# Eight backward mLSTM states beside the Hyena convolution, and the decay applied as the state product leaves its bank

## The chip, the cores and the metric

The kernel runs on one core of a Trainium2 chip. A core has five engines with queues of their own: TensorE (PE, matrix products into the PSUM banks), VectorE (DVE), ScalarE (ACT), GpSimd (POOL, which does not touch PSUM here) and SyncE (SP, which here only issues DMAs). PEld stands for the weight loads of TensorE. The metric is the device time of one execution in microseconds; lower is better.

## The reference

One encoder layer over a sequence of 2048 tokens and 1024 channels. Half of the mixer is a Hyena group (a long two-sided convolution by FFT, applied twice), the other half an mLSTM with four heads of 128 channels, run once forward and once backward over the sequence and summed. Cross-attention into 256 memory tokens, an MLP and norms follow. The part that the change touches is the chunkwise mLSTM; for one direction and one chunk:

```python
def step(carry, inp):
    C, n, m = carry
    qc, kc, vc, ic, fc = inp
    F = jnp.cumsum(fc, axis=-1)
    logw = F[..., :, None] - F[..., None, :] + ic[..., None, :]
    logw = jnp.where(lower, logw, -jnp.inf)
    log_inter = F + m[..., None]
    m_t = jnp.maximum(log_inter, jnp.max(logw, axis=-1))
    w = jnp.exp(logw - m_t[..., None])
    inter = jnp.exp(log_inter - m_t)
    s = jnp.einsum('bhtd,bhsd->bhts', qc, kc) * w
    num = jnp.einsum('bhts,bhse->bhte', s, vc) + inter[..., None] * jnp.einsum('bhtd,bhde->bhte', qc, C)
    den = jnp.sum(s, axis=-1) + inter * jnp.einsum('bhtd,bhd->bht', qc, n)
    h = num / jnp.maximum(jnp.abs(den), jnp.exp(-m_t))[..., None]
    ...
    C_new = carry_decay[..., None, None] * C + jnp.einsum('bhs,bhsd,bhse->bhde', we, kc, vc)
```

The backward direction is the same on the flipped sequence. `inter` is one number for each token and head: the decay by which the product of the queries with the incoming state is scaled.

## The kernel before

The kernel works on chunks of 128 tokens, so there are 16. A state is a 128x129 matrix for each head: column 129 is the normaliser, since the values carry a 129th column of ones (`va`).

The program is written as generators that yield a cost, and `weave` interleaves two of them by those costs; a planner then orders the instructions of each engine. `keep_in_program_order` (often called `pin`) holds an instruction at its place in the written order. In `program`:

- `hyena` (the convolution) is woven with the rest of the input projection (`sweep`, `natural`), with `gates`, which `among` advances by one step after every fourth step of the last sweep, and with the first five steps of `memproj` (`take(n, 5)`), which projects the memory keys and values for attention.
- Then the rest of `memproj` is woven with 20 steps of `mlstm`: 15 backward state updates and the first forward chunks. One more step follows.
- Then `attention` is woven with the remaining forward chunks, and `ffn` ends the kernel.

`gates` computes for all chunks and both directions, from the gate pre-activations, two rows for each direction, chunk and head (`negM`, the negated running maximum, and `inter`, the decay), which it stores to DRAM as `rows` (L1044, L1045), and four sets of columns, turned by TensorE and kept on chip as `cols` (L1052 to L1056).

`mlstm` opens its SBUF pool `m_sb` where the convolution's pool `h_sb` lay, so its first loads wait for the convolution's last tiles. It first runs the backward states from chunk 15 to chunk 1 (L1111 to L1120): load the chunk's keys (`kn`) and values (`va`), weight the values on POOL (`ve`), four products into two PSUM banks (L1102), add to the decayed old state on DVE (L1108; L1104 for the first chunk), and store the state to DRAM as `cbd` (L1118).

The forward loop then takes chunk after chunk. `loads` (L1122) fetches queries, transposed keys, the backward state `cbn`, values and rows, each row broadcast to all 128 partitions (tile `rw`, L1124, 256 KB a load): `negM` for each direction and `inter` where a state comes in. `scores` makes the score product, multiplies the queries by the decay row on POOL (L1156), adds the mask on POOL (L1157), takes the exponential on ACT (L1159) and multiplies by the scores on DVE (L1160). For each direction and pair of heads the products of the weights with the values (L1188) and of the scaled queries with the state (L1190) accumulate in one PSUM bank; ACT takes the absolute value of the normaliser (L1193), DVE forms the divisor and the output (L1196 to L1205).

PSUM banks come from two rings of four: `mm` for the large products, `hy` for the convolution, the mLSTM and attention's transposes. A take from a ring waits until the bank's last reader is done.

Of the kernel before, what the change touches and what calls it, by code (L numbers as in the profile page):

```python
# [9 lines left out]
F32 = mybir.dt.float32  # L10
# [122 lines left out]
class Prog:  # L133
# [821 lines left out]
    def gates_open(self, es):  # L955
        self.mcp = es.enter_context(self.tc.tile_pool(name="m_c", bufs=1, side="right"))
        self.gcols = self.mcp.tile([128, 4, 128], F32, name="cols")

    def gates(self):
        nc, tc = self.nc, self.tc  # L960
        gt = self.dram("gt", (L, 16))
        rows = self.dram("rows", (2, 128, 128))
        cols, pin = self.gcols, tc.keep_in_program_order
        with tc.tile_pool(name="m_g", bufs=1, side="right") as sg:
# [79 lines left out]
            nc.sync.dma_start(out=rows[0], in_=negM)  # L1044
            nc.sync.dma_start(out=rows[1], in_=inter)  # L1045
# [10 lines left out]
            nc.vector.tensor_copy(cols.rearrange("p a r -> p (a r)"), pt)  # L1056
        yield 1

    def mlstm(self, es):
# [4 lines left out]
        vd = self.dram("vd", (L, CH)).rearrange("(n s) c -> s n c", s=128)  # L1064
        od = self.dram("od", (L, CH)).rearrange("(n s) c -> s n c", s=128)
        ym = self.dram("ym", (L, CH))
        rows = self.dram("rows", (2, 128, 128))
# [3 lines left out]
        GC, EC, WC, DC = (cols[:, i] for i in range(4))  # L1071
# [10 lines left out]
        def bc(t, r):  # L1082
            return t[:, r:r + 4].unsqueeze(2).broadcast_to([128, 4, 129])

        def load(n, tag, src, bufs=2):
            t = sb.tile([128, 4, 128], F32, tag=tag, name=tag, bufs=bufs)
            nc.sync.dma_start(out=t.rearrange("p h d -> p (h d)"), in_=src[:, n])
            return t

        def load_v(n):  # L1090
            t = sb.tile([128, 4, 129], F32, tag="va", name="va", bufs=2)
            nc.sync.dma_start(out=t[:, :, 0:128], in_=vd[:, n].rearrange("s (h d) -> s h d", h=4))
            nc.vector.memset(t[:, :, 128:129], 1.0)
            return t

        def update(new, old, kk, va, r, eng):
            ve = sb.tile([128, 4, 129], F32, tag="ve", name="ve", bufs=2)
            eng.tensor_tensor(ve, va, bc(WC, r), ALU.mult)
            for p in range(2):
                pc = self.hy()  # L1100
                for i in range(2):
                    nc.tensor.matmul(pc[:, 129 * i:129 * i + 129], kk[:, 2 * p + i], ve[:, 2 * p + i], start=True, stop=True)  # L1102
                if old is None:
                    nc.vector.tensor_copy(new[:, 2 * p:2 * p + 2].rearrange("d h e -> d (h e)"), pc[:, 0:258])  # L1104
                    continue
# [826 lines left out]
```

## Time and profile before

| | us |
|---|---|
| median of 3 runs | 3234.75 (3233.29 to 3247.62) |
| profiled execution | 3234.7 |
| its span, first to last instruction | 3232.7 |

| engine | busy us | share of the span |
|---|---|---|
| PE | 3061.6 | 95% |
| PEld | 2442.4 | 76% |
| DVE | 2033.0 | 63% |
| ACT | 1506.0 | 47% |
| POOL | 1181.1 | 37% |

Busy time is an average over stages with different limits, so the stage has to be looked at and not the total. A busy TensorE is not TensorE at its peak: the granted clock (PEclk) says how fast it was allowed to run. In lists of transfers and products a name stands for a tile (`rw<-rows` is a load of the tile `rw` from the DRAM tensor `rows`), L1102 for line 1102 of the kernel, SPq for the queue of SyncE. Matmuls on 32-bit floats show as two instructions each.

### The profile page before, as it was taken

To read this page: it belongs to the slowest core of one execution; us is meant where nothing else is said; L and a number is where in the kernel's file an instruction comes from. 1 tells how busy PE (TensorE), PEld (TensorE's weight loads), DVE (VectorE), ACT (ScalarE), POOL (GpSimd) and SP (SyncE) were. 2 spreads that over 40 slices of the span, in tenths; PEclk is the share of its full clock that TensorE was granted. 3 is DMA by queue.
4 is the path that set the end of the run, shared out by engine and by line. 5 is a ranking of instruction groups with operands and counts; after the bars stand their busy time and mean duration, and the time that the engine had idled before them with its cause. 6 is when DMAs were issued, how large, how long until landed. Compare 5 with 4: busy or idle time off the path is not lost.

```text
span 3232.7 us, 45325 instructions
## 1 busy us (share of the span) xinstructions
PE 3061.6 (95%) x15241; PEld 2442.4 (76%) x15241; DVE 2033.0 (63%) x3535; ACT 1506.0 (47%) x2874; POOL 1181.1 (37%) x818
## 2 busy tenths in 40 slices
PE   6999999999999875999999998999999999999998
PEld 5655566776668764898988896888788887888876
DVE  7775366345865754776775556656755675556695
ACT  5533366434674333555453445555555543333335
POOL 0122012100111334324141207776855483434483
PEclk9999999999999996999999999999999999999999
DMA  5564776686666898667484537665644475444434
GB/s 191 186 208 161 248 203 201 178 274 177 194 198 191 274 301 270 204 186 251 132 286 140 186 99 238 210 210 162 216 149 152 160 243 159 137 135 149 125 95 166
DMA packets 451632, 617.71 MB, mean 191 GB/s; under 512 B 39614, under 2 KB 247614, under 8 KB 450376
## 3 DMA queue, kind: packets, MB, share of 16 engines
q1 hardware_dynamic: 415268, 556.31, 55.6%
q10 hardware_dynamic: 36132, 58.51, 5.4%
q8 instruction: 121, 1.98, 0.3%
q14 instruction: 111, 0.91, 0.1%
HBM read 416.47 MB, written 198.21 MB: 190 GB/s over the span
## 4 chain that ended last, share of the span: by engine, by line
PE 75%; DMA 10%; DVE 7%; issue 3%; ACT 2%; POOL 2%; SPq 1%; ACTq 0%; DVEq 0%; POOLq 0%
PE mm L340 16%; PE mm L338 16%; PE mm L339 16%; PE hy L340 5%; PE hy L338 5%; PE hy L339 5%; PE hy L175 3%; PE hy L873 1%; PE mm L842 1%; DMA rw<-rows 1%; PE hy L915 1%; DMA xt<-in_x_t_dram 1%; DVE wl L343 1%; PE hy L1188 1%; DVE bl L1505 1%
## 5 line engine op out<-in xcount | busy, mean ns | idle before, releaser
L343 DVE TENSOR_TENSOR wl<-wn,wh 128x512 fp32r<-128x512 f32 (+1 forms) x364 | 278.7, 802 | 116.6 <-ACT wh L343 116.0
L1505 DVE TENSOR_TENSOR bl<-wr,bh 128x512 fp32r<-128x512 f32 x213 | 236.8, 1118 | 132.0 <-ACT bh L1504 131.8
L1504 ACT CAST ah<-w 128x512 fp32r<-128x512 f32 x284 | 176.2, 622 | 299.8 <-PE hy L339 149.4
L920 POOL TENSOR_TENSOR b<-b,a 128x512 f32<-128x512 f32 x64 | 86.7, 1355 | 595.5 <-ACT b L918 454.9
L343 ACT CAST wh<-wn 128x512 fp32r<-128x512 f32 (+1 forms) x364 | 208.5, 617 | 180.6 <-PE mm L339 51.1
L338 PE MATMUL mm<-xh,wh 128*128 128x512 f32 x640 | 271.9, 426 | 3.0 <-ACT xh L498 2.6
L1505 DVE TENSOR_TENSOR al<-w,ah 128x512 fp32r<-128x512 f32 x236 | 225.0, 955 | 57.2 <-ACT ah L1504 56.8
L339 PE MATMUL mm<-xl,wh 128*128 128x512 f32 x640 | 256.9, 402 | 2.3 <-DVE xl L343 2.0
L340 PE MATMUL mm<-xh,wl 128*128 128x512 f32 x640 | 256.7, 401 | 0.0
L1504 ACT CAST bh<-wr 128x512 fp32r<-128x512 f32 x232 | 143.6, 621 | 234.7 <-PE mm L340 180.0
L340 PE MATMUL mm<-bh,al 128*128 128x512 f32 x576 | 225.3, 394 | 7.7 <-DVE al L1505 5.1
L338 PE MATMUL mm<-bh,ah 128*128 128x512 f32 x576 | 226.6, 393 | 0.1
L339 PE MATMUL mm<-bl,ah 128*128 128x512 f32 x576 | 225.6, 392 | 0.0
L338 PE MATMUL mm<-act,wh 128*128 128x512 f32 x512 | 199.5, 393 | 1.2 <-ACT wh L343 1.2
L339 PE MATMUL mm<-act,wh 128*128 128x512 f32 x512 | 200.3, 391 | 0.0
L340 PE MATMUL mm<-act,wl 128*128 128x512 f32 x512 | 199.0, 392 | 0.3 <-DVE wl L343 0.3
L1361 POOL TENSOR_TENSOR ssum<-ssum,sq 128x512 f32<-128x512 f32 x56 | 81.1, 1448 | 289.5 <-ACT sq L1360 289.5
L338 PE MATMUL hy<-bh,ah 128*128 128x512 f32 x448 | 175.2, 391 | 0.0
L339 PE MATMUL hy<-bl,ah 128*128 128x512 f32 x448 | 174.6, 390 | 0.0
L340 PE MATMUL hy<-bh,al 128*128 128x512 f32 x448 | 174.4, 390 | 0.0
L338 PEld LDWEIGHTS mm<-xh,wh 128*128 128x128 f32 x640 | 121.3, 190 | 63.2 <-issue 29.3
L339 PEld LDWEIGHTS mm<-xl,wh 128*128 128x128 f32 x640 | 121.2, 189 | 52.9 <-issue 24.9
(367 smaller groups left out, 8789.4 us busy)
## 6 DMA issues: line engine op xcount, KB each, us to landing
wr<-hc SPq DMA_DIRECT2D x224, 256.0 KB
w<-in_ff_w_dram SPq DMA_DIRECT2D x176, 256.0 KB
hc<-t SPq DMA_DIRECT2D x128, 256.0 KB
wn<-in_w_in_dram SPq DMA_DIRECT2D x100, 256.0 KB
hc<-q SPq DMA_DIRECT2D x96, 256.0 KB
fs<-a SPq DMA_DIRECT2D x32, 512.0 KB
a<-fs SPq DMA_DIRECT2D x64, 256.0 KB
a<-zs SPq DMA_DIRECT2D x64, 256.0 KB
```

The costliest lines, as they stand in the source:

```text
L175: b = self.nc.tensor.matmul(*products[-1], start=True, stop=True)
L338: mm(ps, lh, rh, start=start, stop=False)
L339: mm(ps, lh, rl, start=False, stop=False)
L340: mm(ps, ll, rh, start=False, stop=stop)
L343: both = (self.nc.scalar.copy(hi, src), self.nc.vector.tensor_tensor(lo, src, hi.bitcast(F32), ALU.subtract))
L842: nc.tensor.matmul(pp, dm[:, m], t[:, m], start=True, stop=True)
L873: nc.tensor.matmul(pg, em[:, m], y, start=True, stop=True)
L915: nc.tensor.matmul(pp, dm[:, m], t[:, m], start=True, stop=True)
L920: nc.gpsimd.tensor_tensor(xt, xt, hi[:, m], ALU.mult)
L1361: nc.gpsimd.tensor_tensor(ssum, ssum, sq, ALU.add)
L1504: self.nc.scalar.copy(hi, src)
L1505: eng.tensor_tensor(lo, src, hi.bitcast(F32), ALU.subtract)
```

## The change

Two things are changed.

First, the backward states of chunks 15 to 8 are computed by a new generator `far_states`, with a small pool of its own (`m_b`), and advanced by one step after every step of the last two `natural` tiles and of the first five steps of `memproj`, so inside the weave with the convolution. Their products are pinned. `mlstm` reloads the last of these states from `cbd` and goes on from chunk 7. `gates` is advanced after every third step instead of every fourth. The weave of `memproj` and `mlstm` takes 13 steps instead of 20 with other costs: 8 backward and 5 forward, where it was 15 and 5.

Second, the decay is no longer loaded as a broadcast row and multiplied into the queries. `inter` is turned into a fifth set of columns. The state product gets a bank of its own (`pt`), with the plain queries; ACT scales it by the decay column while it copies it out (`w`), and DVE adds it to the other product (`u`). What follows reads `u` from SBUF instead of the bank. The ring of the remaining rows grows from four tiles to six.

```diff
     def gates_open(self, es):
-        self.gcols = self.mcp.tile([128, 4, 128], F32, name="cols")
+        self.gcols = self.mcp.tile([128, 5, 128], F32, name="cols")
...
-            nc.sync.dma_start(out=rows[0], in_=negM)
-            nc.sync.dma_start(out=rows[1], in_=inter)
+            nc.sync.dma_start(out=rows, in_=negM)
...
+            pt = self.hy()
+            pin(nc.tensor.transpose(pt[:, 0:128], inter, self.ident))
+            nc.vector.tensor_copy(cols[:, 4], pt[:, 0:128])
...
+    def old_state(self, sb, n):
+        t = sb.tile([128, 4, 129], F32, tag="cf", name="cb", bufs=3)
+        cbd = self.dram("cbd", (15, 128, 516))
+        self.nc.sync.dma_start(out=t.rearrange("d h e -> d (h e)"), in_=cbd[n - 1])
+        return t
+
+    def backward(self, sb, first, last, old, pin=None, lean=False):
+        kn = self.dram("kn", (L, CH)).rearrange("(n s) c -> s n c", s=128)
+        cbd = self.dram("cbd", (15, 128, 516))
+        nxt = self.load_c(sb, first, "kn", kn), self.load_v(sb, first)
+        for n in range(first, last, -1):
+            kk, va = nxt
+            nxt = (self.load_c(sb, n - 1, "kn", kn), self.load_v(sb, n - 1)) if n - 1 > last else None
+            yield 3
+            new = sb.tile([128, 4, 129], F32, tag="cf", name="cb", bufs=2 if lean else 3)
+            self.update(sb, new, old, kk, va, 64 + 4 * n, self.nc.gpsimd, pin, 1 if lean else 2)
+            self.nc.sync.dma_start(out=cbd[n - 1], in_=new.rearrange("d h e -> d (h e)"))
+            old = new
+        yield 3
+
+    def far_states(self):
+        with self.tc.tile_pool(name="m_b", bufs=1, side="right") as sb:
+            yield from self.backward(sb, 15, 7, None, self.tc.keep_in_program_order, True)
...
-        for n in range(15, 0, -1):
...
+        for _ in self.backward(sb, 7, 0, self.old_state(sb, 8)):
             yield 3
...
-                for i in range(2):
-                    if i == 1 and (n == 0, cbn is None)[d]:
-                        continue
-                    t = sb.tile([128, 4, 128], F32, tag=f"r{i}", name="rw", bufs=4)
...
+                t = rows_[d] = sb.tile([128, 4, 128], F32, tag="r0", name="rw", bufs=6)
+                get(out=t.rearrange("p h t -> p (h t)"),
+                    in_=rows[r:r + 4].rearrange("h t -> (h t)").unsqueeze(0).broadcast_to([128, 512]))
...
-                if (d, 1) in rows_:
-                    it = rows_[d, 1]
-                    nc.gpsimd.tensor_tensor(it, it, qn, ALU.mult)
...
+                u = sb.tile([128, 4, 129], F32, tag="u", name="u", bufs=2)
+                for p in range(2):
+                    pt = self.hy() if state is not None else None
+                    pn = self.hy()
+                    for i in range(2):
+                        h, own = 2 * p + i, slice(129 * i, 129 * i + 129)
+                        if state is not None:
+                            nc.tensor.matmul(pt[:, own], qn[:, h], state[:, h], start=True, stop=True)
+                        nc.tensor.matmul(pn[:, own], nm[:, h], va[:, h], start=True, stop=True)
...
+                    w = sb.tile([128, 2, 129], F32, tag="w", name="w", bufs=2)
+                    for i in range(2):
+                        h, own = 2 * p + i, slice(129 * i, 129 * i + 129)
+                        nc.scalar.activation(w[:, i], pt[:, own], AF.Copy, scale=IC[:, r + h:r + h + 1])
+                    nc.vector.tensor_tensor(u[:, 2 * p:2 * p + 2].rearrange("t h e -> t (h e)"),
+                                            w.rearrange("t h e -> t (h e)"), pn[:, 0:258], ALU.add)
+                den = sb.tile([128, 4, 1], F32, tag="den", name="den", bufs=4)
+                dv = den.rearrange("t h o -> t (h o)")
+                nc.scalar.activation(den, u[:, :, 128:129], AF.Abs)
+                nc.vector.tensor_tensor(dv, dv, EC[:, r:r + 4], ALU.max)
...
-                        nc.tensor.matmul(dst, nm[:, h], va[:, h], start=True, stop=state is None)
-                        if state is not None:
-                            nc.tensor.matmul(dst, rows_[d, 1][:, h], state[:, h], start=False, stop=True)
...
-                            p.natural(0, (3,)), among(p.sweep(range(4, 10), 0, False), p.gates(), 4),
-                            p.natural(0, (0, 1), p.prep_mem, 2), take(n, 5)),
+                            p.natural(0, (3,)), among(p.sweep(range(4, 10), 0, False), p.gates(), 3),
+                            among(chain(p.natural(0, (0, 1), p.prep_mem, 2), take(n, 5)), p.far_states(), 1)),
                       279, 499)
             m = p.mlstm(ms)
-            weave(n, take(m, 20), 60, 75)
+            weave(n, take(m, 13), 85, 75)
```

The new `update`, `load_c` and `load_v` do what the functions of the same work did inside `mlstm`, with the pool as an argument.

106 lines of the change are left out of this document (42 added, 64 removed).

## The prediction

> **What bounds the kernel now.** I read the page's first two parts first: busy shares, then the slices, to see which stages TensorE fills and which not. The digits are tenths of one fortieth of the span, 80.8 us each.
>
> ```profile
> span 3232.7 us, 45325 instructions
> PE 3061.6 (95%) x15241; PEld 2442.4 (76%) x15241; DVE 2033.0 (63%) x3535; ACT 1506.0 (47%) x2874; POOL 1181.1 (37%) x818
> ...
> PE   6999999999999875999999998999999999999998
> ...
> PEclk9999999999999996999999999999999999999999
> DMA  5564776686666898667484537665644475444434
> ```
>
> TensorE is the bound nearly everywhere. One valley stands out: slices 14 to 16 (PE 8, 7, 5), where the DMA digits are 8, 9, 8 and, in the last, the granted clock falls to 6. I then took the stretches around it. Columns: busy microseconds of each engine, granted clock, DMA share, GB/s.
>
> ```profile
> core 0: us, PE busy (x) PEld busy (x) DVE busy (x) ACT busy (x) POOL busy (x), PEclk, DMA share, GB/s
> 955.00:1030.00 75.00, 72.88 (x477) 60.20 (x476) 39.25 (x58) 40.10 (x75) 13.87 (x10) 1.00 0.60 169
> 1030.00:1100.00 70.00, 64.83 (x463) 54.05 (x461) 43.84 (x99) 24.46 (x46) 20.93 (x13) 0.98 0.96 286
> 1100.00:1140.00 40.00, 32.66 (x215) 27.25 (x216) 36.45 (x80) 15.78 (x29) 17.89 (x11) 0.96 0.79 256
> 1140.00:1230.00 90.00, 63.68 (x340) 53.03 (x339) 38.37 (x104) 30.30 (x60) 24.59 (x25) 0.83 0.99 305
> 1230.00:1305.00 75.00, 49.10 (x288) 46.30 (x288) 43.45 (x138) 24.83 (x108) 34.87 (x28) 0.73 0.84 263
> 1305.00:1640.00 335.00, 329.30 (x2121) 296.64 (x2122) 239.39 (x622) 167.28 (x455) 95.93 (x71) 1.00 0.63 193
> ```
>
> 955 to 1140 is the end of the Hyena convolution; 1140 to 1230 holds the 15 backward state updates and the last part of the memory projections; 1230 to 1305 the first five forward chunks; from 1305 attention runs beside the other eleven. In the valley (1140 to 1305, 165 us) TensorE is busy 112.8 us, much of it on a slow clock, and no engine comes near full except the DMA: 0.99 for 90 us. The chain that ended last, taken over 1140 to 1320, and the waits of 1145 to 1305 say the same (waits: microseconds in total, times, longest).
>
> ```profile
> by line: DMA rw<-rows 13.3%; DMA kn<-kn 9.2%; DMA wn<-in_xa_wv_dram 8.9%; DMA cbd<-cb 7.1%; DMA va<-vd 5.1%; issue 5.0%; DMA wn<-in_xa_wo_dram 4.6%; DMA qn<-qt 4.5%; PE hy L1102 3.8%; DMA vw<-o 3.5%; PE hy L1188 3.5%; PE mm L338 2.9%; PE hy
> ```
>
> ```profile
> POOL rw L1157 <- DMA rw<-rows: 29.2, 11, 5.3
> POOL ve L1098 <- DMA va<-vd: 26.4, 9, 5.9
> ...
> PE hy L1188 <- DVE ht L1201: 4.7, 2, 4.2
> ```
>
> Transfers lead the chain: the rows broadcast to all partitions (rw), the chunk keys and values (kn, va), the states going out (cbd), the projection weights. So I price the valley in bytes. Its DMA issues, first for 1140 to 1230, then for 1230 to 1305:
>
> ```profile
> DMA packets 25676, 27.45 MB, mean 305 GB/s; under 512 B 1666, under 2 KB 17880, under 8 KB 25671
> ...
> kn<-kn SPq DMA_DIRECT2D x17, 256.0 KB
> va<-vd SPq DMA_DIRECT2D x17, 256.0 KB
> ...
> cbd<-cb SPq DMA_DIRECT2D x15, 258.0 KB
> ...
> rw<-rows SPq DMA_DIRECT2D x8, 256.0 KB
> ```
>
> ```profile
> DMA packets 18084, 19.74 MB, mean 263 GB/s; under 512 B 1104, under 2 KB 11441, under 8 KB 18077
> ...
> rw<-rows SPq DMA_DIRECT2D x21, 256.0 KB
> ```
>
> **The change, part by part.** Durations of the operations that are moved, removed or nearest to the new ones (min/median/max in ns; the second fence is from the chain that ended last: start, microseconds, what):
>
> ```profile
> L1108 DVE SCALAR_TENSOR_TENSOR cb<-cb,cols,hy x56: 334/342/352, 1156.1 to 1218.2; 128x129 f32<-128x129 f32 x56
> L1118 SPq DMA_DIRECT2D cbd<-cb x15: 320/382/1155, 1155.3 to 1221.6; - x15
> L1104 DVE COPY cb<-hy x2: 427/427/427, 1154.0 to 1154.5; 128x258 f32<-128x258 f32 x2
> L1098 POOL TENSOR_TENSOR ve<-va,cols x15: 1046/1048/1498, 1152.2 to 1206.4; 128x516 f32<-128x516 f32 x15
> L1156 POOL TENSOR_TENSOR rw<-rw,qn x30: 1257/1287/1747, 1229.6 to 1576.3; 128x512 f32<-128x512 f32 x30
> L1159 ACT ACTIVATE rw<-rw,cols x128: 384/387/405, 1217.5 to 1581.7; 128x128 f32<-128x128 f32 x128
> L1193 ACT ACTIVATE hy<-hy x64: 148/157/163, 1236.6 to 1637.0; 128x2 f32<-128x2 f32 x64
> L1201 DVE TENSOR_TENSOR ht<-hy,den x32: 394/416/425, 1237.4 to 1619.7; 128x256 f32<-128x256 f32 x32
> L779 ACT COPY st<-mm x32: 368/373/378, 598.7 to 1026.3; 128x256 f32<-128x256 f32 x32
> ```
>
> ```profile
> 1344.64 0.89 PE hy L1102 x8
> ```
>
> (1) *Eight of the fifteen updates leave the valley.* They take 8 x (256 + 256 + 258) KB = 6.31 MB out of 1140 to 1230 and put one state load (0.26 MB) back. Of the eight rw issues there seven fetch chunks 0 and 1, three of these the decay rows: 0.79 MB more. Net 6.83 MB, at that stretch's 305 GB/s 22.4 us. The bounds: 22.4 if bytes pace it, as the share of 0.99 says, and about 10 if the projections' own weights, stores and products keep it long. I take 22, by the share.
>
> (2) *Decay rows.* Of the 21 rw issues of 1230 to 1305 ten are decay rows, 2.62 MB, at 263 GB/s 10.0 us; each also had a POOL product of 1.29 us (L1156). The DMA share there is 0.84 and not 0.99, so bytes pace most of it, not all. I take 8; bounds 0 (another chain) and 10.
>
> (3) *Eight updates enter the convolution.* They are emitted after each step of two projections whose last value store was copied at 1026 (L779) and of the first memory projections, so between about 955 and 1100. TensorE: 0.89 us a step, 7.1 us. It idles only 2.1 + 5.2 us there, so nearly all of it lengthens the stage: 7. DVE: seven steps of four L1108 (0.342) and one of two copies (0.427), 10.4 us; POOL: 8 x 1.05 us; both engines are under two thirds busy there, so that is covered. DMA: 6.31 MB. Up to 1030 the share is 0.60, and 30 us of DMA time are free; about five of the eight pairs of loads and three stores fall there. The rest, some 2.9 MB, or 10 us at 286 GB/s, meets a share of 0.96, where TensorE already waits for weights:
>
> ```profile
> PE mm L340 <- DVE wl L343: 6.3, 9, 1.1
> PE mm L338 <- ACT wh L343: 5.0, 6, 2.1
> ```
>
> Bounds 0 to 10, since a loaded weight tile is used several microseconds later; I take 4. Queues: a cbd store waits on SP for the update's DVE work, with the convolution's loads and the weight loads behind it. Today that wait is small:
>
> ```profile
> SPq L1118 <- DVE cb L1108: 4.5, 8, 1.2
> ```
>
> On POOL a ve product (1.05 us) stands ahead of the convolution's own products. Sixteen more takes of the four "hy" banks, with matmuls fixed in their place, can stop TensorE until DVE has drained a bank. For these together 0 to 8; I take 2, as the waits above are short ones.
>
> (4) *The gates* come a little earlier, with one more transpose and copy and one store less: nothing, at most 1 us.
>
> (5) *Forward chunks, other engines.* Matmul count is unchanged: the state product only gets its own bank. Each chunk gains eight ACT scalings (nearest row: L1159, 0.387) and loses two of four small ACT operations: +2.8 us of ACT. DVE gains four adds over 258 columns (nearest: L1201, 0.416), +1.7 us. POOL loses 2.6 us. From 1305 ACT is busy half its time and DVE 0.71, so I book 0; without that cover it is up to 11 x 1.2 us (two scalings and an add before a bank comes free) = 13. Lighter DMA there can give at most the 5.7 us TensorE idles.
>
> Sum: -22 - 8 + 7 + 4 + 2 = -17. The profiled execution took 3234.7 us (2.0 beyond its span), the median of the runs is 3234.75, so I predict 3217.5, say 3217.
>
> The bytes are priced by the 305 and 263 GB/s of the two rows. The Trainium skill (DMA: Bandwidth & Descriptors, Specifications) gives a limit of some 358 GB/s for memory traffic of one core; an estimate by it makes the same 9.45 MB worth 26 us instead of 32, and the sum 3223; the trace disagrees, with a share of 0.99 already at 305 GB/s.
>
> **The rivals.**
>
> *A. TensorE gets its clock back.* The clock granted is 0.83 and 0.73 in the valley, so its 63.7 + 49.1 us of matmul are 53 + 36 at full clock. If fewer waits let the clock recover, up to 24 us of TensorE time go beyond the bytes; only what lies on the path counts, and there matmuls are a minority. I take 12: 3205. Against it: the remaining waits are still transfers. The Trainium skill (TensorE: Matmul & The Clock Gate, Part 1: The HAM clock gate) says the clock halves after some 3.4 us of idling and returns after as much work; the rows' clock between one half and one agrees.
>
> *B. The bytes only move.* With the far updates gone the projections' weights and stores hold the first stretch, and the valley gives 15 in all; the stage before pays 7 of matmul and the full 10 of its busy DMA: 3237, no change. For it: the share of 0.96 from 1030, and 13.5% of the chain on xa_wv and xa_wo weights. Against it: 0.60 up to 1030.
>
> *C. The "hy" banks become the bound beside attention.* A chunk takes 11 banks in place of 7, from a ring of four: the scores of the next chunk hold one, and now already the fourth product of the first direction needs it back. Attention's transposes use the same ring. If TensorE stops there in each of the eleven chunks, the valley's gain is lost from 17 / 11 = 1.6 us a chunk on; at 3.2 us, waiting for the next chunk's masked rows as well as the drain, it is 35 us: 3252, slower. For it: the wait of L1188 for L1201 quoted above is such a bank wait. Against it: from 1305 TensorE idles only 5.7 of 335 us, and has attention's products to put in between.
>
> **How the numbers follow.** My forecast, 3217 with its own range 3207 to 3226 (from the bounds of 2, 3 and 5), gets 0.42; A 0.18, B 0.22, C 0.18. A half per cent, 16 us, is about what a measurement of this kernel can tell from no change: 3218.5 and 3251 are the limits. Of the forecast's chance I count 0.32 below 3218.5 and 0.10 above. Faster: 0.32 + 0.18 = 0.50; same: 0.10 + 0.22 = 0.32; slower: 0.18. The range takes in A and B and ends short of C's price: 3198 to 3246.
>
> **What would show it.** Steps 1 and 2: the time from the end of the convolution's stores to the first attention product falls from 165 to about 135 us, with seven cb stores in it and half as many rw issues, and the wait of POOL for rw shrinks. Step 3: eight updates between 955 and 1110 and the end of the convolution later by some 13 us. Step 5: 1305 to 1640 keeps its 335 us; if it grows, C. The prediction fails if the valley stays as long with its DMA share falling (then transfers were not what paced it), if the convolution's end slips by over 25 us, or if TensorE's idle time beside attention rises above 15 us.

## The result, and the profile after

The changed kernel takes 3242.28 us (median of 20 runs, 3235.87 to 3249.20). The kernel before, run beside it, takes 3241.28 us (20 runs, 3233.29 to 3248.13). The ratio is 1.0003, with a 95% interval of 0.9996 to 1.0011: no change. Forecast were 3217 us and a gain of half a per cent.

The two profiled executions are not equally typical. The one before (3234.7 us) was 6.5 us quicker than its kernel's median, the one after (3246.2 us) 4 us slower. Some 10 of the 11.5 us between the two traces are therefore chance. Totals below go by the timed runs, and a trace says where time lies, to a few us.

The first two parts of the page of the changed kernel, in the forty slices of 81.1 us each:

```profile
span 3244.5 us, 45267 instructions
...
PE 3058.6 (94%) x15242; PEld 2438.6 (75%) x15242; DVE 2066.6 (64%) x3584; ACT 1529.7 (47%) x2961; POOL 1145.5 (35%) x788
...
PE   6999899999999875999999998999999999999998
...
PEclk9999999999999888999999999999999999999999
DMA  5564777686677997556384527665644475444434
```

The valley is still there (PE 8, 7, 5 in slices 14 to 16). The DMA digits of slices 14 to 18 are 9, 9, 7, 5, 5, where they were 8, 9, 8, 6, 6: busier ahead, emptier behind. The stretches of the prediction, for the changed kernel:

```profile
core 0: us, PE busy (x) PEld busy (x) DVE busy (x) ACT busy (x) POOL busy (x), PEclk, DMA share, GB/s
955.00:1030.00 75.00, 73.02 (x483) 60.68 (x481) 36.93 (x65) 34.80 (x66) 13.62 (x11) 1.00 0.67 194
1030.00:1100.00 70.00, 63.48 (x448) 53.31 (x448) 45.27 (x104) 22.36 (x43) 20.71 (x14) 0.98 0.98 295
1100.00:1140.00 40.00, 33.55 (x190) 25.57 (x189) 33.04 (x72) 11.39 (x21) 17.76 (x11) 0.83 0.78 239
1140.00:1230.00 90.00, 65.30 (x383) 56.24 (x381) 47.55 (x105) 39.01 (x83) 24.15 (x22) 0.89 0.89 274
1230.00:1305.00 75.00, 42.28 (x267) 38.22 (x268) 49.42 (x146) 36.33 (x140) 19.80 (x16) 0.86 0.72 226
1305.00:1640.00 335.00, 325.57 (x2097) 294.31 (x2096) 248.16 (x638) 178.53 (x494) 71.18 (x50) 0.99 0.55 175
```

In 1230 to 1305 the DMA share is 0.72 where it was 0.84, and TensorE does less than before (42.28 us of matmuls for 49.10). These stretches are fixed while the stages moved: the convolution's last store now comes 16 us later and the first attention product 10 us earlier, so each stretch holds other work than before. From that store to that product, before and then after:

```profile
1141.41:1305.09 163.68, 111.38 (x618) 97.92 (x616) 81.10 (x243) 54.55 (x166) 58.58 (x51) 0.78 0.92 286
```

```profile
1157.53:1295.25 137.72, 82.24 (x498) 72.22 (x496) 77.70 (x214) 59.95 (x183) 35.12 (x32) 0.86 0.83 260
```

The DMA share falls there too, from 0.92 to 0.83: the transfers no longer fill it. The issues left as planned. The bytes of 1140 to 1230 fell only from 27.45 to 24.66 MB, since that stretch now begins 17 us before the convolution's last store. The DMA lines for 1140 to 1230, then for 1230 to 1305:

```profile
DMA packets 22276, 24.66 MB, mean 274 GB/s; under 512 B 1488, under 2 KB 15742, under 8 KB 22270
...
kn<-kn SPq DMA_DIRECT2D x9, 256.0 KB
rw<-rows SPq DMA_DIRECT2D x8, 256.0 KB
cbd<-cb SPq DMA_DIRECT2D x7, 258.0 KB
```

```profile
DMA packets 16011, 16.96 MB, mean 226 GB/s; under 512 B 937, under 2 KB 10756, under 8 KB 16004
...
rw<-rows SPq DMA_DIRECT2D x10, 256.0 KB
```

Waits in the valley of the changed kernel (1145 to 1305), and the two new operations from 1180 to 1640 (count, then busy us and mean ns, then idle time before them):

```profile
POOL rw L1169 <- DMA rw<-rows: 67.7, 15, 17.7
...
PE hy L1199 <- DVE bry L214: 9.4, 1, 9.4
```

```profile
L1207 ACT ACTIVATE w<-hy,cols 128x129 f32<-128x129 f32 x120 | 36.6, 363 | 35.7 <-PE hy L1199 31.4 <-DVE u L1208 2.4 <-ACT hg L1467 0.9
...
L1208 DVE TENSOR_TENSOR u<-w,hy 128x258 f32<-128x258 f32 x60 | 24.7, 417 | 15.0 <-PE hy L1200 8.4 <-ACT w L1207 6.4
```

The durations are those of the prediction (0.363 and 0.417 us for the 0.387 and 0.416 taken). New is a stop of TensorE of 9.4 us: the state product wants a "hy" bank that the chunk's root (`bank_rsqrt`, released in L214) holds.

Three moments of each trace carry the comparison from here on: the convolution's last store (`yh`), the first product of attention (`mm<-act`) and its last. The valley is the time between the first two, the attention stage that between the last two (us). The second and third traces of each kernel come from runs of the same program below.

| kernel | last `yh` store | valley | attention stage | both |
|---|---|---|---|---|
| before, three traces | 1141.4, 1147.1, 1141.4 | 163.7, 163.9, 163.0 | 639.3, 639.4, 644.6 | 803.0, 803.3, 807.6 |
| after, three traces | 1157.5, 1154.5, 1156.8 | 137.7, 137.1, 135.7 | 657.6, 654.2, 650.5 | 795.3, 791.3, 786.2 |

So the valley did become some 27 us shorter and the convolution some 13 us longer, as forecast. The attention stage grew by 6 to 18 us, where no change was booked.

### The profile page after: what moved, and what is told of

The parts are those of the page before. It is cut to its first block, busy times and chain, and to the rows that moved or that the text cites. A ratio compares the mean times of both kernels' runs of the same rounds, so it can differ in the third digit from the quotient of the medians.

```text
span 3244.5 us, 45267 instructions
## 1 busy us (share of the span) xinstructions
PE 3058.6 (94%) x15242; PEld 2438.6 (75%) x15242; DVE 2066.6 (64%) x3584; ACT 1529.7 (47%) x2961; POOL 1145.5 (35%) x788
## 4 chain that ended last, share of the span: by engine, by line
PE 73%; DMA 11%; DVE 8%; issue 3%; ACT 3%; POOL 1%; SPq 1%; ACTq 0%; DVEq 0%; POOLq 0%
PE mm L339 15%; PE mm L341 15%; PE mm L340 15%; PE hy L341 5%; PE hy L339 5%; PE hy L340 5%; PE hy L176 3%; PE mm L843 1%; PE hy L874 1%; PE hy L916 1%; DVE wl L344 1%; DVE bl L1520 1%; DMA rw<-rows 1%; DMA xt<-in_x_t_dram 1%; DMA kn<-st 1%
## 5 line engine op out<-in xcount | busy, mean ns | idle before, releaser
L339 PE MATMUL hy<-xh,ah 128*128 128x512 f32 x384 | 151.8, 396 | 9.2 <-ACT ah L1519 8.4
```

The costliest lines, as they stand in the source:

```text
L339: mm(ps, lh, rh, start=start, stop=False)
```

## The experiments

Ratios are to the kernel before, run beside it on the same chip, with 95% intervals. One per cent is 32 us.

### Both kernels again, and each half alone

The first two runs are the two kernels unchanged, for second traces. The third keeps all backward states in `mlstm` and takes only the decay columns; the fourth takes only the far states, with the decay rows as before.

```diff
 # decay columns alone
-            weave(n, take(m, 20), 60, 75)
+            weave(n, take(m, 21), 60, 78)
...
+                    nc.scalar.activation(w[:, i], pt[:, own], AF.Copy, scale=IC[:, r + h:r + h + 1])
...
 # far states alone
-                            p.natural(0, (0, 1), p.prep_mem, 2), take(n, 5)),
+                            among(chain(p.natural(0, (0, 1), p.prep_mem, 2), take(n, 5)), p.far_states(), 1)),
...
-        for n in range(15, 0, -1):
+        for _ in self.backward(sb, 7, 0, self.old_state(sb, 8)):
```

> The kernel before, unchanged, for a second trace of it. The first trace (3234.7 us) lies 6.5 us under the median of 20 runs, so it was a quick execution. All theories expect the same stage times within 3 us each: the convolution's last store near 1141, the first attention product near 1305, the first product of the MLP near 1944. If a stage differs by more, stage differences of that size between single traces mean nothing.

> The changed kernel, unchanged, for a second trace of it. In the first, the convolution ends 16 us later than before, the first attention product comes 10 us earlier, and the first MLP product 8.5 us later, with 6.6 + 3.7 us of TensorE waiting for POOL's sums (L1376). If the loss beside attention belongs to the change, it is there again (8 to 18 us from the first attention product to the first MLP product); if it was that execution alone, it is gone and the MLP starts at about the same time as before.

> The second part alone: decay columns and own banks, all 15 backward updates where they were. Theory 1 (bytes pace the valley, and what is moved is paid elsewhere): the valley loses about 3.4 MB of decay rows and nothing is paid in the convolution, so 8 to 11 us faster, near 3231 when before is 3241. Theory 2 (the valley is paced by the round trip of loads that are issued only when a buffer comes free): about as before, within 4 us. Theory 3 (the banks or the longer chain on ACT and DVE cost it back beside attention): the valley gains and the attention stage loses, together 5 to 15 us slower.

> The first part alone: eight backward updates beside the convolution, decay rows loaded as before. Theory 1: the valley gives some 22 us, the convolution pays 7 of matmul and the bytes that meet busy DMA, some 10, so 0 to 8 us faster. Theory 2: the backward steps are round trips too, so the valley shortens by about what the convolution pays, within 4 us of before. Theory 3: 10 to 17 us faster, since it is the other part that loses.

Measured: 3242.9 us and 3238.96 us for one execution each of the kernels before and after. The decay columns alone: 3248.93 us, ratio 1.0036 (1.0023 to 1.0050). The far states alone: 3224.81 us, ratio 0.9958 (0.9942 to 0.9973), quicker than both kernels.

The halves add up: +0.36% and -0.42% make the result. The gain is real and belongs to the far states (valley 138.0 us, last store at 1159.0), and the other half loses all of it. With the decay columns alone the valley stayed at 160.7 us, though no decay rows were loaded in it. In the decay-only trace, TensorE's waits of 1145 to 1305 are led by the bank of the root:

```profile
PE hy L1199 <- DVE bry L214: 17.3, 2, 10.5
PE hy L1165 <- DMA kk_t<-kt: 9.2, 1, 9.2
PE hy L1165 <- DMA qn<-qt: 9.0, 2, 6.7
```

### What in the second half costs: banks, ScalarE, or buffers

Three runs of the whole change with one suspect taken away each: the root computed in SBUF, so that it takes no bank; the scaling moved from ScalarE to VectorE; three buffers instead of two for queries, backward states and values. A fourth makes the edit of the root in the kernel before, as a control.

```diff
 # root without a bank
-                rv = self.bank_rsqrt(sb, ss, 128)
+                ms = sb.tile([128, 8], F32, tag="ms", name="ms", bufs=2)
+                nc.vector.tensor_scalar(ms, ss, 1.0 / 128, EPS, ALU.mult, ALU.add)
+                rv = self.rsqrt(sb, ms, "mr")
...
 # scaling on VectorE
-                        nc.scalar.activation(w[:, i], pt[:, own], AF.Copy, scale=IC[:, r + h:r + h + 1])
+                    nc.vector.tensor_tensor(w, pt[:, 0:258].rearrange("t (h e) -> t h e", h=2),
+                                            IC[:, r + 2 * p:r + 2 * p + 2].unsqueeze(2).broadcast_to([128, 2, 129]), ALU.mult)
...
 # three buffers
-            qn = sb.tile([128, 4, 128], F32, tag="qn", name="qn", bufs=2)
+            qn = sb.tile([128, 4, 128], F32, tag="qn", name="qn", bufs=3)
```

> The changed kernel, but the mLSTM's inverse root (a chain of 13 small DVE operations after each second chunk) works in SBUF and no longer holds a hy bank. Theory A (the ring of four hy banks became tight: with 11 takes a chunk in place of 7 the long-held bank comes round sooner, as in the stall of 10.45 us of the decay-only trace behind L214): the stalls of TensorE behind L214 and L1238 go, 5 to 12 us faster than the changed kernel, so near 3232 when that is 3242. Theory B (the eight scalings in ACT's queue hold back the weight splits) and theory C (loads that wait for a buffer pace the valley): within 3 us of the changed kernel.

> The same edit on the kernel before, as a control. Theory A: with 7 takes a chunk the ring is not tight, or less so: 0 to 4 us faster than before. If it gains as much here as in the changed kernel, the held bank is no part of what the change cost.

> The changed kernel with the scaling done by one DVE product for each pair of heads in place of two ACT operations: 64 ACT operations less for each direction, 32 DVE operations more. Theory B: 4 to 10 us faster than the changed kernel, with smaller waits of PE for the weight splits (wh) in the valley. Theory A: about the same or up to 4 us slower, since the banks are still taken and DVE, the busier engine, empties them. Theory C: the same within 3 us.

> The changed kernel with three buffers in place of two for queries, values and backward states in the mLSTM, so that these loads are issued a chunk earlier. Theory C: the waits for va and qn in the valley go and the first attention product comes 5 to 15 us earlier than in the changed kernel. Theories A and B, and bytes as the bound: within 3 us, since no byte, bank or ACT operation less is needed.

Measured: root without a bank 3232.97 us, 0.9989 (0.9978 to 1.0000); its control 3244.09 us, 1.0020 (1.0009 to 1.0032); scaling on VectorE 3242.67 us, 1.0019 (1.0005 to 1.0033); three buffers 3237.21 us, 0.9999 (0.9986 to 1.0013).

Moving the scaling off ScalarE wins nothing, and neither does a third buffer. Theories B and C fall. (In the trace with three buffers the valley is shorter, 130.2 us, but the attention stage takes 656.8 us and the time is the same.) The root's bank is worth 0.14% to the changed kernel, some 5 us, and the stop of 9.4 us is gone from its trace (valley 127.3 us); the same edit brings nothing before the change. That speaks for theory A, a ring of banks that has become tight, but it is a small part of what is missing, and hardly more than the spread measured next.

### The planner's order, no own banks, and earlier far states

In the changed kernel TensorE stopped for 3.7 us at 1665 us, where a GpSimd product of the memory sums stood ahead of an addition that TensorE waited for. One edit was meant to start those sums a step later, with a control before the change. A third run takes the own banks and the scaling away (and with them the decay, which it leaves out). The fourth lays the far states earlier, beside the last memory sweep.

```diff
 # sums later (after, and before)
-        sums = [None] * 20 + list(range(4))
+        sums = [None] * 21 + list(range(4))
...
 # no own banks, no scaling
-                            nc.tensor.matmul(pt[:, own], qn[:, h], state[:, h], start=True, stop=True)
-                        nc.tensor.matmul(pn[:, own], nm[:, h], va[:, h], start=True, stop=True)
+                        nc.tensor.matmul(pn[:, own], nm[:, h], va[:, h], start=True, stop=state is None)
...
+                            nc.tensor.matmul(pn[:, own], qn[:, h], state[:, h], start=False, stop=True)
+                    nc.vector.tensor_copy(u[:, 2 * p:2 * p + 2].rearrange("t h e -> t (h e)"), pn[:, 0:258])
...
 # far states alone, earlier
-                            p.natural(0, (3,)), among(p.sweep(range(4, 10), 0, False), p.gates(), 3),
-                            among(chain(p.natural(0, (0, 1), p.prep_mem, 2), take(n, 5)), p.far_states(), 1)),
+                            p.natural(0, (3,)),
+                            among(chain(p.sweep(range(4, 10), 0, False), p.natural(0, (0, 1), p.prep_mem, 2)),
+                                  chain(p.gates(), p.far_states()), 2), take(n, 5)),
```

> The changed kernel with the memory sums' queue started one planner step later (21 empty steps for 20), so that a product of that queue no longer stands ahead of the attention sums' add in GpSimd's order near 1660 us. Theory D, the order written by the planner: the changed chunks shifted that order, and TensorE's stop of 3.7 us at 1665 with the slow clock behind it is its price; about 6 us faster than the changed kernel (3236), and no wait of over 1.5 us of TensorE for that add between 1640 and 1680. Rival, the banks alone: the same time as the changed kernel (3242), the stop goes elsewhere.

> The changed kernel with the state product accumulated into the scores' own bank, as before the change, and without the scaling by the decay columns, which this run leaves out altogether: no extra bank, no ScalarE scaling, one VectorE copy a pair. Far states and the missing decay rows stay. Theory A, the own banks cost what the change loses beside attention: 8 to 14 us faster than the changed kernel (3228 to 3234), and the attention stage takes about 643 us as in the run with the far states alone. If the decay rows' bytes are worth anything by themselves, it ends below the run with far states alone (3225), by up to 8 us; if they are worth nothing, at about 3225. Rival, the order of the planner: no more than 4 us faster than the changed kernel.

> The far states alone (decay rows as before), started earlier: gates and far states are laid between the last memory sweep and the next projections, two to a step, so that they are through before the stretch from 1030 to 1100 us where the DMA share is 0.96 or more. Theory 1, the moved updates cost the convolution what their transfers take from the weights' there: 5 to 10 us faster than the run with far states alone, 3215 to 3220, the convolution's last store at 1150 or earlier. Rival, they cost what their products and banks take: the same, 3225, the last store at 1159.

> Control for the run with later memory sums: the kernel before with the same shift of one step. Theory D, the shift only undoes a bad order that the change made: no change (3239, within 3 us). Rival, a later queue is good for any kernel: as many us faster as the changed kernel is with it.

Measured: sums later, after the change 3238.03 us, 1.0014 (1.0004 to 1.0023); before it 3235.98 us, 1.0016 (1.0001 to 1.0031); no own banks 3234.51 us, 1.0002 (0.9992 to 1.0011); far states earlier 3222.18 us, 0.9968 (0.9957 to 0.9978).

The shift of the sums changed nothing. The planner wrote both programs as they had been, instruction for instruction on every engine, so these two runs are repeats. As such they are worth having: the kernel before measured 1.0016 of itself, and the changed kernel 1.0014 after 1.0003. Differences below some 0.2% between single kernels are not read from here on. What the order at 1665 costs stays untried.

Taking the own banks away did not bring back the 0.4% expected. Its trace does have the attention stage that was expected with it, 644.1 us. That holds for every trace on record: the seven with own banks take 649.2 to 657.6 us there, whichever engine scales, and the thirteen without them 637.3 to 646.9 us. So own banks and scaling go with some 10 us more beside attention in the traces, of which the timed runs show 4 (1.0002 here, 1.0014 for the changed kernel run beside it).

Laying the far states earlier ended the convolution at 1140.7 us, and yet the time is that of the far states alone within the spread: which of transfers and products the convolution pays for stays open.

### Rows and copy, separately

What is left of the second half is that decay rows are neither loaded nor multiplied, and that products are copied out of the bank into a tile (`u`), from which denominators and output come. The four combinations, run together on one chip, all with far states and without own banks. Where the rows are absent the decay is left out of the computation. Some differences ride along. Without rows the ring of the remaining rows has six tiles. With the copy, the absolute value and the first direction's output are made in one operation for all four heads. And the run with neither rows nor use in the bank keeps the changed kernel's `gates` with the fifth set of columns, where the other three have four sets.

```diff
 # rows kept, products copied out
-                    pvs.append(pn[:, 0:258].rearrange("t (h e) -> t h e", h=2))
-                    nc.scalar.activation(pn[:, 260 + 2 * p:262 + 2 * p].unsqueeze(2), pv[:, :, 128:129], AF.Abs)
+                    nc.vector.tensor_copy(u[:, 2 * p:2 * p + 2].rearrange("t h e -> t (h e)"), pn[:, 0:258])
...
+                nc.scalar.activation(den, u[:, :, 128:129], AF.Abs)
...
 # no rows, products used in their bank
-                            nc.tensor.matmul(dst, rows_[d, 1][:, h], state[:, h], start=False, stop=True)
+                            nc.tensor.matmul(dst, qn[:, h], state[:, h], start=False, stop=True)
...
-                if (d, 1) in rows_:
-                    it = rows_[d, 1]
-                    nc.gpsimd.tensor_tensor(it, it, qn, ALU.mult)
```

> The far states with the decay rows as before, but each pair's products are copied out of their bank by VectorE into a tile, and denominators and output are made from the tile, as in the changed kernel. Theory E, the copy and the chain behind it cost: about 0.4% slower than the far states alone, at 1.000 of the kernel before. Theory F, the missing decay rows cost by changing when other transfers run: as the far states alone, 0.996. Theory G, single runs of one program differ between sessions by this much: as the far states alone, and the two corners of this call differ by less than 0.2%.

> The far states, with the decay rows not loaded and not multiplied into the queries: the state product takes the queries themselves, so the decay is left out of the computation, and everything else of a chunk is as before. This is the worth of the rows by themselves, which the prediction put at 8 us. Theory E: faster than the far states alone by 0 to 8 us, 0.994 to 0.996. Theory F: slower than the far states alone by some 10 us, 0.999 to 1.000. Theory G: as the far states alone or up to 8 us faster.

> The far states alone, once more, as the first corner of this call. Theories E and F: 0.996 as it measured. Theory G: 0.998 or more, as near to the other corner as to its own first result.

> The changed kernel without own banks and scaling (the decay left out of the computation), once more, as the second corner. Theories E and F: 1.000 as it measured, 0.4% above the far states alone. Theory G: within 0.2% of the far states alone.

Measured:

| | decay rows loaded | no decay rows |
|---|---|---|
| used in the bank | 3230.32 us, 0.9963 (0.9949 to 0.9977) | 3215.37 us, 0.9923 (0.9910 to 0.9936) |
| copied to a tile | 3232.56 us, 0.9978 (0.9968 to 0.9989) | 3235.57 us, 0.9987 (0.9977 to 0.9996) |

This tells most of the parts apart. Theory F falls, since leaving the rows out gains by itself, and theory G can't give the second corner of the first row. Theory E has the right part, but its price appears only in one column. The rows are worth 0.40%, 13 us, as long as the products are used in their bank. The copy costs 0.15% (not more than the spread) while the rows are loaded, and 0.64%, 21 us, once they are not. From the convolution's last store to the first attention product, one trace each: far states alone, the same copied out, without rows, without rows and copied out:

```profile
1155.83:1291.55 135.72, 95.20 (x532) 82.77 (x530) 68.17 (x201) 52.38 (x164) 51.19 (x43) 0.80 0.93 290
```

```profile
1154.84:1292.02 137.18, 93.57 (x533) 81.55 (x532) 81.02 (x216) 49.86 (x146) 50.80 (x43) 0.83 0.93 288
```

```profile
1159.27:1283.43 124.16, 88.87 (x530) 77.01 (x529) 67.64 (x202) 53.70 (x162) 35.42 (x32) 0.89 0.92 294
```

```profile
1156.52:1293.95 137.43, 86.19 (x500) 77.09 (x498) 75.42 (x215) 49.66 (x147) 35.02 (x32) 0.83 0.83 259
```

The valley takes 135.7, 137.2, 124.2 and 137.4 us, and the attention stage behind it changes little (644.9, 646.9, 641.2 and 642.4 us): what the rows gave, the copy took, in the valley. In the first three the DMA share is 0.92 or 0.93, so the transfers fill it with and without rows. Only without rows and with the copy does the share fall, to 0.83. That fits a valley that takes the longer of its transfers and of the work from chunk to chunk, with the copy hidden as long as the transfers are the longer. It is a reading of four traces, and the differences named above are not tested apart.

In the last one TensorE waits longest there for a chunk's queries (waits of 1195 to 1300):

```profile
PE hy L1165 <- DMA qn<-qt: 16.0, 2, 11.8
```

### Which part of the copy

Both runs leave the rows and the decay out. The first adds copies that nobody reads. The second makes the output from them, but takes the denominators from the bank.

```diff
 # copies that nobody reads, added to the run without rows
+                    nc.vector.tensor_copy(u[:, 2 * p:2 * p + 2].rearrange("t h e -> t (h e)"), pn[:, 0:258])
                     pvs.append(pn[:, 0:258].rearrange("t (h e) -> t h e", h=2))
...
 # and the output from the copies
-                        nc.vector.tensor_tensor(y[:, hp], pv[:, :, 0:128], den[:, hp].broadcast_to([128, 2, 128]), ALU.mult)
+                        nc.vector.tensor_tensor(y[:, hp], u[:, hp, 0:128], den[:, hp].broadcast_to([128, 2, 128]), ALU.mult)
...
```

> The far states without the decay rows (the decay is left out of the computation, as in the run whose label begins e14), and beside it each pair's products are copied by VectorE into a tile that nobody reads. Denominators and output come from the bank. Theory H, the longer chain from the products over the copy to denominators and output costs: 0.992 to 0.993, as without the copies. Theory I, the copies themselves cost, as VectorE's in-order work ahead of the next step: 0.997 to 0.999. Theory J, the planner writes another order whenever a chunk's instructions change, and orders differ: anything from 0.992 to 1.000, with no relation to which instruction was added.

> As the run before it (the decay left out of the computation), but the output is made from the copied tile, and the denominators from the bank, so the chain from the products to the denominators doesn't pass the copy. Theory H: 0.994 to 0.996 if the denominators' way over the copy carried most, 0.998 if the output's did. Theory I: 0.997 to 0.999, as with the copies alone. Theory J: apart from the run with copies alone by any sign, by up to 0.4%.

Measured: copies alone 3218.51 us, 0.9939 (0.9922 to 0.9957); output from the copies 3221.12 us, 0.9943 (0.9928 to 0.9958).

The copies cost some 5 us, no more than the spread, and the output made from them nothing that can be told. (In the two traces the valley is 132.2 and 133.0 us, longer than the 124.2 without copies, and the attention stage 637.3 and 637.9 us, shorter than 641.2.) The step to 0.9987 comes only where the denominators are made from the tile too. That run differs in two more things, the fifth set of columns and the single operations for four heads. The extra product for the columns runs at 893 us, long before the valley, but neither of these two, nor the denominators, was tested by itself. Theory H gave this number, but not for its reason. In these two runs ScalarE's absolute value waits for the copy as well, since both touch the same bank (waits of 1195 to 1300, first run, then second):

```profile
ACT hy L1205 <- DVE u L1202: 15.4, 8, 6.7
```

```profile
ACT hy L1205 <- DVE u L1202: 17.6, 6, 6.9
```

So the chain over the copy is as long there, and it alone doesn't cost the 0.4%. What differs visibly is the order of work at the valley's entry. In the traces of the changed kernel (three), of the kernel without own banks (two), and with the root in SBUF or the scaling on VectorE (one each), ScalarE stands still for 2.3 to 4.8 us before a row's exponentials. The profile puts this down to the store of the last backward state (`cbd`). A weight cast stands behind the exponentials, and TensorE stops for 4.7 to 8.4 us for that cast. No other trace has this wait of ScalarE. Why an exponential should wait for that store is not shown. Between the last store of a backward state and the first product of a chunk pass 18.3 to 19.4 us in the seven traces that have it, and 11.5 to 13.0 us in the runs without rows that use the bank for their denominators, and in the kernel before. For 1195 to 1216 of the kernel without own banks, then TensorE for 1195 to 1219 of the kernel with the denominators from the bank:

```profile
ACT rw L1171 <- DMA cbd<-cb: 4.8, 1, 4.8
```

```profile
PE mm L339 <- ACT wh L344: 10.7, 2, 8.3
```

```profile
PE mm L339 <- ACT wh L344: 3.3, 1, 3.3
```

That is about 6 us of the 14 by which the trace without own banks is longer than the one without rows that uses the bank. It can't be all, for the run with three buffers has the whole change, lacks this wait (9.1 us from the store to the first product), and is no quicker (0.9999). The planner writes another order, far from the chunk too, whenever a chunk's instructions change, so theory J (the order written, not the instruction) is not excluded for the rest: the trace with denominators from the bank wins its time beside attention (637.9 us), the one without copies in the valley (124.2 us). What the denominators themselves cost stays open.

## Why the prediction was wrong

Of the 25 us between 3217 and 3242.28, 6.5 lie in the starting point: the prediction took the median of three runs, 3234.75, where twenty gave 3241.28. The rest is a gain of 17 us that did not come. By the prediction's own steps, with the runs that measure them:

| step | forecast, us | measured |
|---|---|---|
| (1) and (3), far states leave the valley and enter the convolution | -22 + 13 = -9 | far states alone: 0.9958 and 0.9963, -14 and -12 |
| (2) decay rows | -8 (0 to 10) | 0.9963 to 0.9923: -13, only with the products used in the bank |
| (4) gates | 0 (to 1) | not measured by itself |
| (5) forward chunks, other engines | 0 (to 13) | 0.9923 to 1.0003: +26, the gates' fifth columns among it |

**Steps 1 and 3 were right in their sum.** The valley lost 26 to 28 us in the traces of the changed kernel, against 22 and, with the rows, 30 forecast, and the convolution's last store came some 13 us later, as said. The far states alone already take the valley to 138.0 and 135.7 us, so in the changed kernel the share of the rows is missing. Which of its terms the convolution pays for is open. The working held to some 5 us where a transfer was on the path: bytes by the rate of that stretch. One queue was missing in step 3: SP's loads of the next keys wait for the previous chunk's products. In 955 to 1140 of the changed kernel that is its longest wait, though what it costs is not shown:

```profile
SPq L1064 <- PE hy L1082: 20.5, 3, 11.4
```

**Step 2 was right alone and wrong in company.** The rows' bytes were on the path, and their removal is worth a little more than the bound of 10 us allowed. That holds while the transfers still fill the valley without them (share 0.92). With the copy they don't (0.83), and the gain is gone. Rival A's sign, a faster clock, shows in the fixed stretches only (0.89 and 0.86, up from 0.83 and 0.73), and these hold other work than before. Over the valley itself the granted clock is 0.78, 0.77 and 0.80 in the three traces before, and 0.86, 0.81 and 0.78 after.

**Step 5 is the one that failed.** It summed the added work rightly (+2.8 us of ACT, +1.7 us of DVE, durations as measured), then asked for cover only from 1305 on, beside attention: "so I book 0". The runs put 26 us in its place, by the timed runs 21 with the copies (0.9923 to 0.9987) and 5 with own banks and scaling.

One part lies in the valley, where five of the sixteen chunks run. There the copy and what hangs on it take back 13 us in the traces (124.2 to 137.4), where step 2 had just taken away the transfers that hid it: with the rows still loaded, the same copy leaves the valley at 137.2 us for 135.7. This part the step never priced. The other part lies beside attention, where cover was assumed. The stage takes 650.5 to 657.6 us in the changed kernel and 642.4 and 644.1 us without own banks and scaling. The bound of 13 us, eleven chunks without cover, comes near these 11 us, but by luck: of TensorE's waits there only some 2 us are for a bank of these products, on which that bound was built. The prediction's own range left the bound out as well, for 13 us alone would have made its upper end 3230 and not 3226. Which of the added operations carries the price in the valley stays open.

**Rival B** gave nearly the time that came (3237), but not by its mechanism: moving the bytes did gain 0.4%. **Rival C** named the place and the direction, but its mechanism is not shown. Own banks and scaling together cost from 0.9987 or 1.0002 (without them, two runs) to 1.0003 or 1.0014 (with them, two runs), some 5 us and no more than the spread, and the attention stage is longer in every trace that has them. But the one long bank wait, 9.4 us, lies in the valley. Beside attention TensorE's waits of 1305 to 1955 are for the attention's sums, its transposes and loads; none of a microsecond or more is for a state product's bank but the fifth row. Why the stage grows, by the order of the engines or otherwise, was not taken apart. First the changed kernel, then without own banks:

```profile
PE hy L1448 <- POOL ssum L1376: 6.6, 1, 6.6
PE hy L1337 <- DVE act L344: 4.3, 1, 4.3
PE hy L1492 <- POOL ssum L1376: 3.7, 1, 3.7
PE hy L1337 <- DMA wn<-ym: 3.0, 4, 1.5
PE hy L1199 <- DVE ht L1238: 1.6, 2, 1.4
```

```profile
PE hy L1439 <- POOL ssum L1367: 3.9, 1, 3.9
PE hy L1328 <- DVE act L344: 3.5, 1, 3.5
PE hy L1197 <- DVE ht L1229: 2.5, 1, 2.5
```

**Of the signs named**, those of steps 1 to 3 came true but for one: GpSimd's wait for the rows was to shrink, and grew from 29.2 to 67.7 us (57.7 and 37.4 in the other two traces). A wait of an engine that has less to do says nothing on the path. The sign for a failure, more than 15 us of TensorE idle beside attention, did not show in 1305 to 1640, which holds 325.57 us of matmuls for 329.30, 9.4 us of idling for 5.7. Over the whole of attention, 1305 to 1955, it did show: 20.5 us of idling for 12.1, and the five rows above come to 19.2.

## What to carry to other kernels

When a change takes away the transfers that pace a stage and lengthens the work they hid, price the second part as if the first had already been made: cover has to be looked for in the stretch as it will be. Ask for each added instruction in which stage every one of its occurrences runs, not where most of them do. Where a change moves the stages, compare between moments of the program, since fixed stretches hold other work afterwards. And split a change that does two things before shipping it: here one half alone is 0.4% quicker than both kernels, and the other half takes it back.

## What was not expected

- One and the same program differs from itself by 0.16% here between sets of runs (the kernel before measured 1.0016 of itself, interval 1.0001 to 1.0031), more than an interval of ten runs suggests; single traces of one program differ by 9 us between the convolution's last store and attention's last product (795.3, 791.3 and 786.2 us after the change).
- An edit of a few instructions of one chunk changes the order of work far away from it. Taking the own banks away changes ScalarE's order from 1023 us on, VectorE's from 1062 and TensorE's from 1225. Four kernels that differ in their chunk code have the wait of ScalarE before an exponential (2.3 to 4.8 us, seven traces), the others do not.
- A load that had been hidden for the whole chunk before (the queries, `qn`) became the longest stop of TensorE in the valley (11.8 us) in the kernel without own banks, where the queries are kept until the chunk's products and the products come later. In the changed kernel, three buffers instead of two did not pay (0.9999, for 1.0003 of the change).
